# Strassen's block products for the gate projection too, in four of eleven groups of a ConvFFN, with the down projection in six parts instead of four

## The chip, the cores and the metric

One core of one Trainium2 chip runs the whole kernel. The metric is device microseconds of that core from the start to the end of one execution; lower is better. Times are medians of several runs, and each profile is of one execution.

## The reference, cut to what matters

A trunk of two layers, 512 tokens of width 1024 (D), float32. Each layer is a mixer and then a gated ConvFFN of width 2816:

```python
def gated_conv_ffn(x, w_gate, w_up, conv_w, conv_b, w_down):
    g = jnp.einsum('bsd,df->bsf', x, w_gate)
    g = causal_dwconv3(g, conv_w) + conv_b
    up = jnp.einsum('bsd,df->bsf', x, w_up)
    return jnp.einsum('bsf,fd->bsd', jax.nn.silu(g) * up, w_down)
...
        h = h + jnp.einsum('bse,ed->bsd', mix, w_out_even[i])
...
        hn = rms_norm(h, norm_ffn[layer])
        h = h + gated_conv_ffn(hn, w_ffn_gate[layer], w_ffn_up[layer], conv_ffn[layer],
                               b_conv_ffn[layer], w_ffn_down[layer])
    return rms_norm(h, final_norm)
```

The mixer of layer 0 joins a short gated convolution with causal pooling; that of layer 1 is a chunked spatial gate. Both begin with an RMS norm.

## The kernel before

**Arithmetic.** Each float32 operand is split into a high and a low part of a reduced-precision type (fp32r), and each product is three matmuls: high by high, high by low, low by high (`mm3`, L134). High parts are made by ScalarE (a copy), low parts by VectorE (a subtraction, `parts`, L127), or, in `summed` (L118), by ScalarE and an accumulating DMA that GpSimd issues. Weights come on SyncE's DMA queue into four raw buffers, and their halves take turns in five buffers of high and five of low parts.

**An FFN.** Its 2816 channels are 22 tiles of 128. The kernel goes through them in groups of two tiles, f and f + 1 (`hidden`, L711). A group makes the gate and the up projection of its tiles, and from them two activations: the gate gets a convolution over three tokens (`conv`, one ScalarE step L504 and two VectorE steps L506) and a silu (L512), and is multiplied by the up projection; `act` (L515) then splits it into a_hi (ScalarE, L261) and a_lo (VectorE, L263). Six pairs of such buffers take turns.

There are three forms of group:

- f = 0, `direct` (L532): gate and up of both tiles as 96 matmuls of 512 columns, on h not yet normalized, for the norm's factor r is not there when they begin. The factor is applied in `evacuate`: VectorE multiplies the gate by r (L555), GpSimd the silu (L558), VectorE puts in the up projection (L561). Ahead of that evacuation in the program stands `normalize` (L566) for four pairs of 128-row blocks. It makes the normalized halves hgh and hgl, and the sums of blocks (t23, t41) that Strassen's products need.
- f = 2, `direct` again, 96 matmuls of 512 columns, on the normalized halves (copies L553 on ScalarE instead of L555).
- all others, `seven` (L608): the up projection of two tiles by Strassen's seven block products, with 2 x 2 blocks of weights, rows and tokens. A product is 12 matmuls of 256 columns (L663), so 84 in all, where the direct form has 48 of 512 columns. The sums of weight blocks are made on VectorE (L631 to L639) and split (L619, L620). The gate of the same tiles is direct, 48 matmuls of 512 columns, between the first products. Results are gathered from PSUM by ScalarE copies (`keep`, L681) and VectorE additions (`add`, L684).

After each part of the tiles a down projection adds to the result, with all the part's activations as its inner dimension: `project` (L287) for layer 0, into h; a loop with `group8` (L948) for layer 1, into y. A part begins and ends eight PSUM banks, which VectorE adds into h or y (L306 and L923). The parts are

```python
    PARTS = ((0, 6), (6, 12), (12, 18), (18, 22))
```

so the order on TensorE is direct(0), direct(2), seven(4), down; seven(6), seven(8), seven(10), down; and so on.

**What sets the order.** The program is written in the order above, and a scheduler of the framework gives each engine its fixed list; an engine takes its list in order. PSUM has seven banks that matmuls take in turn and one more. The last inner steps of a group (`tail`) run bank by bank, the earlier ones inner step by inner step.

**Mixer 0's norm.** `Norm.rstd` (L194) sums squares over the 128 partitions by two matmuls of 512 columns with a matrix of ones (L200, L201), and takes the root and a reciprocal over 512 columns on VectorE. The FFN's norms use `rstd_tokens` (L206: eight one-column matmuls, then root and reciprocal of four columns) and `rstd_spread` (L215: four transposes that spread the columns over the partitions). `z_done` (L400) evacuates a group's projection and pools it.

Of the kernel before, what the change touches and what calls it, by code (L numbers as in the profile page):

```python
# [8 lines left out]
F32 = mybir.dt.float32  # L9
# [6 lines left out]
P = 128  # L16
# [14 lines left out]
def tile_trunk(ctx: ExitStack, tc: tile.TileContext, x, norm_mix, norm_ffn, final_norm,  # L31
# [16 lines left out]
    def aux_bank(name):  # L48
        return ps_aux.tile([P, 512], F32, tag="aux", name=name)
# [10 lines left out]
    small = cp.tile([P, LINE], F32, name="small")  # L60
    ones = small[:, :1]
    nc.gpsimd.memset(ones, 1.0)
    ones_r = cp.tile([P, P], F32R, name="ones_r")
    nc.gpsimd.tensor_copy(ones_r, ones.to_broadcast([P, P]))
# [20 lines left out]
    def params(layer, rows_, queue=nc.sync):  # L85
        rows = sum(n for _, _, n in rows_)
        pk = cp.tile([P, P], F32, tag="pk", bufs=1, name=f"pk{layer}")
        at, views = 0, {}
        for key, ap, n in rows_:
            queue.dma_start(pk[at : at + n, :], ap)  # L90
            views[key] = at
            at += n
        ps = aux_bank(f"prm_ps{layer}")
        nc.tensor.transpose(ps[:, :rows], pk[:rows, :], ident[:rows, :rows])
        sb = cp.tile([P, P], F32, tag=f"prm{layer}", name=f"prm{layer}")
# [21 lines left out]

    def summed(raw, a, b, name):  # L118

        hi = wp.tile([P, a, b], F32R, tag="whi", bufs=5, name=f"whi_{name}")  # L120
        lo = wp.tile([P, a, b], F32R, tag="wlo", bufs=5, name=f"wlo_{name}")
        nc.scalar.activation(lo, raw, AF.Copy, scale=-1.0)  # L122
        nc.gpsimd.dma_start(lo, raw, accum_op=ALU.add)  # L123
        nc.scalar.activation(hi, raw, AF.Copy)
        return hi, lo

    def parts(raw, a, b, name):  # L127
        hi = wp.tile([P, a, b], F32R, tag="whi", bufs=5, name=f"whi_{name}")
        lo = wp.tile([P, a, b], F32R, tag="wlo", bufs=5, name=f"wlo_{name}")
# [38 lines left out]
    class Norm:  # L168
# [13 lines left out]
        def square(self, k, order=lambda ins: ins):  # L182
            if self.n == 0:
                order(nc.scalar.activation(self.ssq, h[k], AF.Square))
            elif self.n == NK - 1 and self.apart:
                self.last = tp.tile([P, S], F32, tag="last", bufs=1, name=f"last_{self.name}")
                order(nc.scalar.activation(self.last, h[k], AF.Square))
            else:
                sq = tp.tile([P, S], F32, tag="sq", name=f"sq_{self.name}{k}")
                order(nc.scalar.activation(sq, h[k], AF.Square))  # L190
                nc.gpsimd.tensor_tensor(self.ssq, self.ssq, sq, ALU.add)
            self.n += 1

        def rstd(self):  # L194
            ps = aux_bank(f"ss_{self.name}")
            hi = tp.tile([P, S], F32R, tag="sq", name=f"ssh_{self.name}")
            lo = tp.tile([P, S], F32R, tag="sq", name=f"ssl_{self.name}")
            nc.scalar.activation(hi, self.ssq, AF.Copy)
            nc.vector.tensor_tensor(lo, self.ssq, hi.bitcast(F32), ALU.subtract)
            nc.tensor.matmul(ps, ones_r, hi, start=True, stop=False)  # L200
            nc.tensor.matmul(ps, ones_r, lo, start=False, stop=True)  # L201
            r = tp.tile([P, S], F32, tag="rstd", name=f"rstd_{self.name}")
            inv_sqrt(r, ps, S, self.name)
            return r

        def rstd_tokens(self):  # L206

# [139 lines left out]
    def mixer0():  # L347
        nonlocal prm0
        w = w_in_even[0]
        with tc.tile_pool(name="m0", bufs=1) as mp:  # L350
            prm_mix = params("mix", [("mix", rows_of(norm_mix[0]), NK)], nc.scalar)
            norm = Norm("m0", lambda k: prm_mix("mix", k))
            zchunks = {}
            xt = {}

# [12 lines left out]
            def turn(k):  # L368
# [2 lines left out]
                    nc.tensor.transpose(ps[:, t * P : (t + 1) * P], xt[k][:, t, :], ident)  # L371
                if k in raws:
                    raw, a, b, name = raws.pop(k)
                    hi = wp.tile([P, a, b], F32R, tag="whi", bufs=5, name=f"whi_{name}")
                    lo = wp.tile([P, a, b], F32R, tag="wlo", bufs=5, name=f"wlo_{name}")
# [21 lines left out]
            pooled = {}  # L397
            rstd = [None]

            def z_done(g, ps):  # L400
                if rstd[0] is None:
                    rstd[0] = norm.rstd()
                win = WINDOWS[g]
                z = mp.tile([P, S + LINE], F32, tag="z", bufs=2, name=f"z{g}")[:, :W]
                nc.gpsimd.memset(z[:, :PAD], 0.0)
                nc.scalar.copy(z[:, PAD:], ps)
# [80 lines left out]
    class Ffn:  # L487
# [110 lines left out]
        def moving(self, product, kp):  # L598
# [6 lines left out]
                return tuple(t[:, product - 6, :] for t in self.t23[kp])  # L605
            return tuple(t[:, {4: 0, 5: 1}[product], :] for t in self.t41[kp])

        def seven(self, f):  # L608
            layer, ap, n = self.layer, self.ap, f"{self.layer}_{f}"
            raws = ffn_weights(layer, f, [(key, half) for key in "ug" for half in range(2)])  # L610
# [1 line left out]
            stat = {}  # L612

            def pair(name):
                return [wp.tile([P, 2, 4, P], F32R, tag=f"w{x}", bufs=5, name=f"w{x}_{name}_{n}")
                        for x in ("hi", "lo")]

            def halves(hi, lo, src):
                nc.scalar.activation(hi, src, AF.Copy)  # L619
                nc.vector.tensor_tensor(lo, src, hi.bitcast(F32), ALU.subtract)  # L620

            def put(product, hi_lo, i):
                stat[product] = hi_lo[0][:, i], hi_lo[1][:, i]
# [22 lines left out]
                c = slice(i * P, (i + 1) * P)  # L646
                stat[product] = hi[:, :, c], lo[:, :, c]

            BANK = {1: "a", 6: "a", 7: "a", 4: "a", 5: "e", 3: "e", 2: "b"}
            banks, opened = {}, set()  # L650

            def multiply(product):
                at = BANK[product]
                if at not in banks:
                    banks[at] = mm_bank(f"u{at}{n}")
                ps = banks[at][:, :HALF]
                hi, lo = stat[product]
                for kp in range(NP):
                    b_hi, b_lo = self.moving(product, kp)
                    a_hi, a_lo = hi[:, kp, :], lo[:, kp, :]  # L660
                    for l, r, end in ((a_hi, b_hi, False), (a_hi, b_lo, False),
                                      (a_lo, b_hi, kp == NP - 1)):
                        nc.tensor.matmul(ps, l, r, start=at not in opened, stop=end,  # L663
                                         skip_group_check=True)
                        opened.add(at)
                return ps

            def gates(half):
                for k in PAIRS[half * 4 : half * 4 + 4]:
# [41 lines left out]
        def hidden(self, f, before=lambda i, j: None):  # L711
# [235 lines left out]

    def group8(name, ks, lhs, rhs, tail, on_done):  # L948
        banks = {}
        head = len(ks) - tail  # L950
# [43 lines left out]
```

## Time and profile before

| | |
| --- | --- |
| median of 3 runs | 1012.66 us (1012.38 to 1012.75) |
| the profiled execution's own time | 1013.46 us |
| its span between first and last instruction | 1011.5 us |
| mean granted TensorE clock | 0.997 |
| busy: TensorE, VectorE, ScalarE, GpSimd | 998.6, 612.6, 471.5, 90.0 us |
| direct(0) in layer 0 ends, direct(2) begins on TensorE | 171.21 us |
| direct(2) ends, seven(4) begins | 193.14 us |
| last matmul begins | 1003.57 us |

The profile gives the busy time of each engine as a share of the span; the chain of work that ended last, followed back from the end to what released each step; and groups of instructions by line, tile and shape. PE is TensorE, DVE VectorE, ACT ScalarE, POOL GpSimd and SP SyncE. In a timeline each row is the start, the length, the engine, the line, and what is written from what. Matmuls overlap, so the distance of their starts, not their length, is what one costs.

### The profile page before, as it was taken

Reading aid. Unit: us, or ns where it says so; the run is one execution under the profiler, and the core shown is the slowest. Engines: PE = TensorE matmul, PEld = TensorE weight load, DVE = VectorE, ACT = ScalarE, POOL = GpSimd, SP = SyncE. Lnnn points to the kernel's source line nnn. Section 1 sums busy time; section 2 is a strip of 40 time slices with the busy share of each in tenths; the row PEclk is TensorE's granted clock in tenths of the full one; section 3 lists DMA queues with packets and bytes.
Section 4 is the critical chain, followed back from the end, with each engine's and each line's share of the span. In section 5 each row is a group of like instructions: output and inputs, shape, how many; then the busy total and the mean of one; then the engine's idle time right before and its main releaser. Section 6 shows DMA issues by size and latency. Waiting matters only on the chain.

```text
span 1011.5 us, 13009 instructions
## 1 busy us (share of the span) xinstructions
PE 998.6 (99%) x5169; PEld 853.3 (84%) x5169; DVE 612.6 (61%) x882; ACT 471.5 (47%) x685; POOL 90.0 (9%) x101
## 2 busy tenths in 40 slices
PE   9999999999999999999999999999999999999997
PEld 6788888888998899889878888888888988998885
DVE  5997458864557366636833645396745654763667
ACT  6423446642454266236645444575425623650553
POOL 3141021200000000000300001111000000000000
PEclk9999999999999999999999999999999999999998
DMA  7432235442444344434333123354424433442432
GB/s 239 151 104 84 84 99 143 113 146 71 125 117 143 87 119 132 126 84 125 131 120 104 63 90 98 96 121 117 146 63 126 135 116 89 141 127 82 122 87 83
DMA packets 79303, 114.98 MB, mean 114 GB/s; under 512 B 4004, under 2 KB 53388, under 8 KB 79244
## 3 DMA queue, kind: packets, MB, share of 16 engines
q1 hardware_dynamic: 73580, 98.96, 30.7%
q0 software_dynamic: 4320, 13.63, 7.3%
q10 hardware_dynamic: 1344, 1.58, 0.5%
q8 instruction: 40, 0.66, 0.3%
q14 instruction: 19, 0.16, 0.1%
HBM read 98.42 MB, written 2.10 MB: 99 GB/s over the span
## 4 chain that ended last, share of the span: by engine, by line
PE 95%; DVE 3%; ACT 1%; issue 1%; DMA 1%; POOL 0%; DVEq 0%; ACTq 0%; POOLq 0%
PE ua L663 10%; PE g L135 7%; PE g L136 6%; PE g L137 6%; PE ue L663 5%; PE d L136 4%; PE dn L137 4%; PE dn L135 4%; PE d L137 4%; PE d L135 4%; PE dn L136 4%; PE gu L135 3%; PE gu L137 3%; PE gu L136 3%; PE ub L663 3%; PE u L135 1%
## 5 line engine op out<-in xcount | busy, mean ns | idle before, releaser
L135 PE MATMUL g<-hgh,whi_g 128*128 128x512 f32 x288 | 112.5, 391 | 0.0
L136 PE MATMUL g<-hgl,whi_g 128*128 128x512 f32 x288 | 112.5, 391 | 0.0
L137 PE MATMUL g<-hgh,wlo_g 128*128 128x512 f32 x288 | 112.1, 389 | 0.0
L130 ACT ACTIVATE whi_g<-raw_g 128x1024 fp32r<-128x1024 f32 x40 | 42.1, 1053 | 93.6 <-PE dn L137 57.3
L136 PE MATMUL d<-a_lo,whi_d 128*128 128x512 f32 x176 | 68.6, 390 | 0.0
L135 PE MATMUL dn<-whi_dn,a_hi 128*128 128x512 f32 x176 | 68.6, 390 | 0.0
L136 PE MATMUL dn<-wlo_dn,a_hi 128*128 128x512 f32 x176 | 68.5, 389 | 0.0
L506 DVE SCALAR_TENSOR_TENSOR c<-rows,prm,c 128x512 f32<-128x512 f32 x88 | 68.1, 793 | 0.6
L137 PE MATMUL d<-a_hi,wlo_d 128*128 128x512 f32 x176 | 68.5, 389 | 0.0
L137 PE MATMUL dn<-whi_dn,a_lo 128*128 128x512 f32 x176 | 68.3, 389 | 0.0
L135 PE MATMUL d<-a_hi,whi_d 128*128 128x512 f32 x176 | 68.3, 390 | 0.0
L131 DVE TENSOR_TENSOR wlo_g<-raw_g,whi_g 128x1024 fp32r<-128x1024 f32 x40 | 48.8, 1221 | 28.3 <-ACT whi_g L130 28.3
L137 PEld LDWEIGHTS g<-hgh,wlo_g 128*128 128x128 f32 x288 | 54.1, 188 | 11.9 <-DVE wlo_g L131 0.5
L123 POOL DMA_DIRECT2D wlo_u<-raw_u x18 | 15.4, 857 | 536.3 <-ACT wlo_u L122 200.1
L135 PEld LDWEIGHTS g<-hgh,whi_g 128*128 128x128 f32 x288 | 54.2, 188 | 10.3
L136 PEld LDWEIGHTS g<-hgl,whi_g 128*128 128x128 f32 x288 | 54.2, 188 | 9.8
L620 DVE TENSOR_TENSOR wlo_a<-raw_u,whi_a 128x512 fp32r<-128x512 f32 x18 | 12.5, 692 | 82.6 <-ACT whi_a L619 82.6
L681 ACT COPY kept<-ua 128x256 f32<-128x256 f32 x54 | 19.8, 367 | 74.3 <-PE ua L663 74.3
L131 DVE TENSOR_TENSOR wlo_d<-raw_d,whi_d 128x1024 fp32r<-128x1024 f32 x22 | 26.9, 1221 | 35.1 <-ACT whi_d L130 35.1
L131 DVE TENSOR_TENSOR wlo_dn<-raw_dn,whi_dn 128x1024 fp32r<-128x1024 f32 x22 | 26.8, 1220 | 35.1 <-ACT whi_dn L130 35.1
L923 DVE TENSOR_TENSOR y<-dn,y 128x512 f32<-128x512 f32 x32 | 22.1, 689 | 42.9 <-PE dn L137 42.9
L619 ACT ACTIVATE whi_s<-s 128x1024 fp32r<-128x1024 f32 x36 | 38.1, 1057 | 19.9 <-PE d L136 14.2
(326 smaller groups left out, 2756.7 us busy)
## 6 DMA issues: line engine op xcount, KB each, us to landing
raw_u<-in_w_ffn_up_dram SPq DMA_DIRECT2D x36, 512.0 KB
raw_g<-in_w_ffn_gate_dram SPq DMA_DIRECT2D x36, 512.0 KB
raw_d<-in_w_ffn_down_dram SPq DMA_DIRECT2D x22, 512.0 KB
raw_dn<-in_w_ffn_down_dram SPq DMA_DIRECT2D x22, 512.0 KB
wlo_u<-raw_u POOLq DMA_DIRECT2D x18, 512.0 KB, 4.6
raw_oe<-in_w_out_even_dram SPq DMA_DIRECT2D x8, 512.0 KB
raw_g<-in_w_ffn_gate_dram SPq DMA_DIRECT2D x16, 256.0 KB
raw_u<-in_w_ffn_up_dram SPq DMA_DIRECT2D x16, 256.0 KB
```

What stands on the lines that cost most here:

```text
L123: nc.gpsimd.dma_start(lo, raw, accum_op=ALU.add)
L130: nc.scalar.activation(hi, raw, AF.Copy)
L131: nc.vector.tensor_tensor(lo, raw, hi.bitcast(F32), ALU.subtract)
L135: nc.tensor.matmul(ps, lhs[0], rhs[0], start=start, stop=False)
L136: nc.tensor.matmul(ps, lhs[0], rhs[1], start=False, stop=False)
L137: nc.tensor.matmul(ps, lhs[1], rhs[0], start=False, stop=stop)
L506: nc.vector.scalar_tensor_tensor(c, t[:, i : S + i], prm("cf", i * NF + ft), c, op0=ALU.mult, op1=ALU.add)
L619: nc.scalar.activation(hi, src, AF.Copy)
L620: nc.vector.tensor_tensor(lo, src, hi.bitcast(F32), ALU.subtract)
L663: nc.tensor.matmul(ps, l, r, start=at not in opened, stop=end, skip_group_check=True)
L681: nc.scalar.copy(kept[:, i, :], ps)
L923: nc.vector.tensor_tensor(dst, ps, dst, ALU.add)
```

## The change

In groups 6, 10, 14 and 18 of each layer the gate is made by seven block products too (`both`): 168 matmuls of 256 columns in place of 84 of 256 and 48 of 512. Its block sums, their halves and its gathering from PSUM are like those of the up projection, and the products of gate and up alternate. `seven` remains for groups 4, 8, 12, 16 and 20, and shares its helpers with `both`. The parts become six, the first with tiles 0 and 1 alone; each of the others holds four tiles. The weight halves get six buffers instead of five, the activations four instead of six. In `group` and `group8` the part ahead of the tail may be empty. Mixer 0's norm takes the form with `rstd_tokens` and `rstd_spread`; the first two of its four groups are copied out of PSUM and pooled once the factor is there.

```diff
-        hi = wp.tile([P, a, b], F32R, tag="whi", bufs=5, name=f"whi_{name}")
-        lo = wp.tile([P, a, b], F32R, tag="wlo", bufs=5, name=f"wlo_{name}")
+        hi = wp.tile([P, a, b], F32R, tag="whi", bufs=6, name=f"whi_{name}")
+        lo = wp.tile([P, a, b], F32R, tag="wlo", bufs=6, name=f"wlo_{name}")
...
-        head = len(ks) - tail
+        head = max(0, len(ks) - tail)
...
-        def rstd(self):
...
-            norm = Norm("m0", lambda k: prm_mix("mix", k))
+            norm = Norm("m0", lambda k: prm_mix("mix", k), apart=True)
...
             def z_done(g, ps):
-                if rstd[0] is None:
-                    rstd[0] = norm.rstd()
...
+                if g == 0:
+                    norm.rstd_tokens()
+                elif g == 2:
+                    rstd[0] = norm.rstd_spread()
+                    z_pool(0)
+                    z_pool(1)
+                z_copy(g, ps)
+                if g > 1:
+                    z_pool(g)
...
-    PARTS = ((0, 6), (6, 12), (12, 18), (18, 22))
+    PARTS = ((0, 2), (2, 6), (6, 10), (10, 14), (14, 18), (18, 22))
+    BOTH = (6, 10, 14, 18)
...
-            self.acts[ft] = split(self.ap, s, f"a{self.layer}_{ft}", tag="a", bufs=6)
+            self.acts[ft] = split(self.ap, s, f"a{self.layer}_{ft}", tag="a", bufs=4)
...
+        def both(self, f):
...
+            w = self.unit(f"a11_{n}")
+            for i, key in enumerate("gu"):
+                self.halves(w[0][:, i], w[1][:, i], raws[key, 0][0][:, :, :P])
+                put(key, 1, w, i)
+            for key in "gu":
+                r0, r1 = raws[key, 0][0], raws[key, 1][0]
...
+                nc.vector.tensor_tensor(s12[:, 0], r0[:, :, P:], r1[:, :, P:], ALU.add)
+                nc.vector.tensor_tensor(s12[:, 1], s12[:, 0], r0[:, :, :P], ALU.subtract)
+                w = self.unit(f"s12{key}_{n}")
+                self.halves(*w, s12)
...
+                nc.vector.tensor_tensor(s34[:, 0], r0[:, :, :P], r0[:, :, P:], ALU.subtract)
+                nc.vector.tensor_tensor(s34[:, 1], r1[:, :, :P], s12[:, 1], ALU.subtract)
+                hi, lo = summed(*raws[key, 1])
...
+                w = self.unit(f"s34{key}_{n}")
+                self.halves(*w, s34)
...
+            for key, product in (("g", 1), ("u", 1), ("g", 5), ("g", 6), ("u", 5), ("u", 6),
+                                 ("g", 2), ("g", 7), ("u", 2), ("u", 7), ("g", 4), ("g", 3),
+                                 ("u", 4), ("u", 3)):
+                after(key, product, self.multiply(banks[key], f"{key}{n}", product,
+                                                  stat[key, product]))
+                if (key, product) == ("g", 4):
+                    s[1] = self.silu(self.conv(pads[1], f + 1), f + 1)
+                elif (key, product) == ("g", 3):
+                    s[0] = self.silu(self.conv(pads[0], f), f)
...
             elif f == 2:
                 self.direct(2, True, ((0, 1), (2, 3)), self.ch)()
+            elif f in BOTH:
+                self.both(f)
             else:
                 self.seven(f)
```

Here `after` copies a gate's or up's product out of PSUM into the padded rows or into `kept` (ScalarE), or adds it there (VectorE).

More of the change, by code (lines that the diff above doesn't have):

```diff
@@ L62, in tile_trunk @@
     nc.gpsimd.memset(ones, 1.0)
-    ones_r = cp.tile([P, P], F32R, name="ones_r")
-    nc.gpsimd.tensor_copy(ones_r, ones.to_broadcast([P, P]))
     def params0():
@@ L94, in params @@
         nc.tensor.transpose(ps[:, :rows], pk[:rows, :], ident[:rows, :rows])
-        sb = cp.tile([P, P], F32, tag=f"prm{layer}", name=f"prm{layer}")
+        sb = cp.tile([P, P], F32, tag="prm0" if layer == "0" else "prm1", name=f"prm{layer}")
         nc.vector.tensor_copy(sb[:, :rows], ps[:, :rows])
@@ L127, in parts @@
     def parts(raw, a, b, name):
-        hi = wp.tile([P, a, b], F32R, tag="whi", bufs=5, name=f"whi_{name}")
-        lo = wp.tile([P, a, b], F32R, tag="wlo", bufs=5, name=f"wlo_{name}")
+        hi = wp.tile([P, a, b], F32R, tag="whi", bufs=6, name=f"whi_{name}")
+        lo = wp.tile([P, a, b], F32R, tag="wlo", bufs=6, name=f"wlo_{name}")
         nc.scalar.activation(hi, raw, AF.Copy)
@@ L185, in square @@
             elif self.n == NK - 1 and self.apart:
-                self.last = tp.tile([P, S], F32, tag="last", bufs=1, name=f"last_{self.name}")
+                self.last = tp.tile([P, S], F32, tag="rstd", name=f"last_{self.name}")
                 order(nc.scalar.activation(self.last, h[k], AF.Square))
@@ L192, in square @@
             self.n += 1
-        def rstd(self):
[L195 to L204, printed above, removed]
         def rstd_tokens(self):
@@ L373, in turn @@
                     raw, a, b, name = raws.pop(k)
[L374 to L375 removed]
+                    hi = wp.tile([P, a, b], F32R, tag="whi", bufs=6, name=f"whi_{name}")
+                    lo = wp.tile([P, a, b], F32R, tag="wlo", bufs=6, name=f"wlo_{name}")
                     for i in range(a):
@@ L398, in mixer0, with z_copy, z_pool @@
             rstd = [None]
-            def z_done(g, ps):
-                if rstd[0] is None:
-                    rstd[0] = norm.rstd()
[L403 to L406, printed above, removed]
+            zs = {}
+            def z_copy(g, ps):
+                zs[g] = mp.tile([P, S + LINE], F32, tag="z", bufs=2, name=f"z{g}")[:, :W]
+                nc.gpsimd.memset(zs[g][:, :PAD], 0.0)
+                nc.scalar.copy(zs[g][:, PAD:], ps)
+            def z_done(g, ps):
+                if g == 0:
[7 more added lines that the diff above has]
+                    z_pool(g)
+            def z_pool(g):
+                win, z = WINDOWS[g], zs[g]
                 nc.vector.tensor_tensor(z[:, PAD:], z[:, PAD:], rstd[0], ALU.mult)
@@ L606, in moving, with multiply @@
             return tuple(t[:, {4: 0, 5: 1}[product], :] for t in self.t41[kp])
+        BANK = {1: "a", 6: "a", 7: "a", 4: "a", 5: "e", 3: "e", 2: "b"}
+        def multiply(self, banks, name, product, weights_):
+            at = self.BANK[product]
+            first = at not in banks
+            if first:
+                banks[at] = mm_bank(f"{name}{at}")
+            ps = banks[at][:, :HALF]
+            hi, lo = weights_
+            for kp in range(NP):
+                b_hi, b_lo = self.moving(product, kp)
+                a_hi, a_lo = hi[:, kp, :], lo[:, kp, :]
+                for l, r, end in ((a_hi, b_hi, False), (a_hi, b_lo, False),
+                                  (a_lo, b_hi, kp == NP - 1)):
+                    nc.tensor.matmul(ps, l, r, start=first, stop=end, skip_group_check=True)
+                    first = False
+            return ps
@@ L614, in pair @@
             def pair(name):
[L615 to L620, printed above, removed]
+                return self.unit(f"{name}_{n}")
+            halves = self.halves
             def put(product, hi_lo, i):
@@ L647, in seven @@
                 stat[product] = hi[:, :, c], lo[:, :, c]
-            BANK = {1: "a", 6: "a", 7: "a", 4: "a", 5: "e", 3: "e", 2: "b"}
-            banks, opened = {}, set()
+            banks = {}
             def multiply(product):
[L653 to L666, printed above, removed]
+                return self.multiply(banks, f"u{n}", product, stat[product])
             def gates(half):
@@ L949, in group8 @@
         banks = {}
-        head = len(ks) - tail
+        head = max(0, len(ks) - tail)
         order = [(i, j) for i in range(head) for j in range(8)]
```

48 lines of the change are left out of this document (added).

## The prediction

> **What bounds the kernel now.** I read the page's busy shares, then the chain of work that ended last, then the waits of the matrix engine, then the timelines around the end of the first FFN part.
>
> ```profile
> PE 998.6 (99%) x5169; PEld 853.3 (84%) x5169; DVE 612.6 (61%) x882; ACT 471.5 (47%) x685; POOL 90.0 (9%) x101
> ...
> PE 95%; DVE 3%; ACT 1%; issue 1%; DMA 1%; POOL 0%; DVEq 0%; ACTq 0%; POOLq 0%
> ```
>
> TensorE is busy 99% of the span and is 95% of the chain; VectorE has 39% to spare. The waits of TensorE, in full:
>
> ```profile
> PE wst L764 <- POOL ws L757: 1.5, 1, 1.5
> PE clock L56 <- DVE idle L53: 1.3, 1, 1.3
> PE z L135 <- ACT hgh L382: 1.0, 2, 0.8
> PE z L136 <- DVE hgl L384: 0.8, 1, 0.8
> PE xt_ps L371 <- DMA xt<-in_x_dram: 0.7, 1, 0.7
> ```
>
> None lies in an FFN. So fewer matmul microseconds pay in full, and a new wait costs in full. The last part and the way out (last matmul at 1003.57) keep their code.
>
> **Seven products for the gate.** Prices from the chain and the PE timeline:
>
> ```profile
> 206.94 1.43 PE ua L663 x12
> 208.37 1.44 PE ue L663 x12
> 209.81 1.44 PE ub L663 x12
> ...
> ```
>
> Products follow one another at 1.437 us for twelve 256-column matmuls, 0.1198 us each. 512-column ones start 0.2275 apart (171.21, 171.44, 171.67 below). A group's direct gate is 48 x 0.2275 = 10.91 us; its seven products are 84 x 0.1198 = 10.06. Saving 0.85 a group, with 4 groups in each of 2 layers **-6.8 us**. A row of the trace prices both forms, so the ends are narrow: -6.4 to -7.2 by reading the intervals a hundredth either way. The Trainium skill (TensorE: Matmul & The Clock Gate, Wait — 56ns, not 53.3ns?) counts a back-to-back matmul as its columns at 2.4 GHz plus 2.5 ns; by that estimate 48 x 0.2158 - 84 x 0.1092 is 1.19 a group and the sum would be 2.7 us lower. The trace has both forms longer, and decides.
>
> What this adds elsewhere must fit beside TensorE. From the DVE rows of such groups (128x1024 subtraction 1.22 us, 128x512 0.69, 256 columns 0.42, convolution step 0.79), a new group takes DVE 8 x 0.69 (sums) + 0.69 x 2 + 4 x 1.22 (low halves) + 4 x 0.79 + 6 x 0.42 (PSUM into rows) + 2 x 0.42 + 0.69 + 2 x 0.69 = 20.4 us, ACT some 16.4, against 168 x 0.1198 = 20.1 on PE. The group after it takes DVE 15.7 against PE 21.0, the down product of four tiles 10.4 against 21.9: 46.5 of 63 us. So DVE averages 74%, and I cost the steady state at 0. Its tight spot is the seven-product group behind a new one: ACT must copy the first product out 6.9 us after that group starts, behind about 26.9 us of queued work reckoned from the new group's start, where 27.0 are to be had. Ends: 0 to 1.5 us in each of eight places.
>
> **Six parts instead of four.** The number of down matmuls is the same. Two more parts in each layer add 16 PSUM evictions of 0.69 us on DVE a layer, beside other matmuls: 0. POOL's added accumulating copies (0.86 each, one for the gate's half per new group) and SP's reordered weight loads lie beside work too: DMA engines are about half busy. The short first part is another matter. Before, direct(2) stood behind direct(0):
>
> ```profile
> 170.99 0.39 PE L137 MATMUL gu<-hgh,wlo_u 128*128 128x512 f32 x1
> 171.21 0.39 PE L135 MATMUL gu<-hgh,whi_g 128*128 128x512 f32 x1
> 171.44 0.39 PE L136 MATMUL gu<-hgl,whi_g 128*128 128x512 f32 x1
> ```
>
> Those 96 matmuls (21.9 us, to 193.14) hid everything that VectorE, ScalarE and GpSimd then did: the rest of `normalize`, and direct(0)'s evacuation. The instruction order of the changed kernel has on PE direct(0), then the 48 matmuls of the down product of tiles 0 and 1, and only then direct(2). TensorE takes its queue in order, and direct(2)'s banks also come behind the down product's in the rotation of seven. So the down product asks for activation 0 at 171.2. When is it there? These rows of DVE, ACT and POOL give it:
>
> ```profile
> 157.04 1.41 DVE L571 SCALAR_TENSOR_TENSOR x<-h,prm,rstd_f 128x512 f32<-128x512 f32 x2 [4.10 <-ACT rstd_f L222]
> ...
> 175.34 0.69 DVE L555 TENSOR_TENSOR rows<-gu,rstd_f 128x512 f32<-128x512 f32 x1
> ...
> 184.39 0.68 DVE L561 TENSOR_TENSOR s<-gu,s 128x512 f32<-128x512 f32 x1
> ...
> 188.62 0.68 DVE L561 TENSOR_TENSOR s<-gu,s 128x512 f32<-128x512 f32 x1
> ```
>
> ```profile
> 179.84 1.28 ACT L512 ACT_TABLE_LOAD   x1
> 181.13 0.72 ACT L512 ACTIVATE s<-c,prm 128x512 f32<-128x512 f32 x1
> ...
> 185.10 0.63 ACT L261 ACTIVATE a_hi<-s 128x512 fp32r<-128x512 f32 x1 [1.05 <-DVE s L561]
> ```
>
> ```profile
> 181.94 1.98 POOL L558 TENSOR_TENSOR s<-s,rstd_f 128x512 f32<-128x512 f32 x1 [1.50 <-ACT s L512]
> ```
>
> From 157.04 DVE is full with `normalize` until the first evacuation at 175.34; then convolution, table load, silu, POOL's product, DVE's, and a_hi ends at 185.10 + 0.63 = 185.7. The changed order on DVE has the same `normalize` ahead of the same L555; down weights (two subtractions of 1.22) take the place of group 4's (0.69 + 1.22 + 2 x 0.69). So TensorE stands still from 171.2 to about 185.8, **14.6 us**. The low half comes at 187.0; activation 1 has silu at 185.75, POOL 1.58, DVE 0.68, ACT 0.62, low half at about 190.3, and 38 of the 48 matmuls remain then: 38 x 0.2275 = 8.65. direct(2) starts at about 199.0, instead of 171.2 + 10.9 with no wait. Loss 199.0 - 182.1 = **16.9 us**. Layer 1 has the same offsets (direct(2) from 673.02, its a_hi at 686.90: 13.9 behind, as in layer 0), so **+33.8** for both. Ends near it: direct(2)'s copies and convolution steps (1.05 on ACT, 1.40 and 1.78 on DVE) no longer stand between, which may give back 1.4 us a layer: +31; the two down weight copies now among `normalize`'s halves on ACT may cost 1.1 each layer: +36. Far end: the evacuation ahead of `normalize`, by its rows 0.69 + 0.72 + 2 x 0.79 + 1.28 + 0.72 + 1.98 + 0.68 + 0.63 = 8.3 us, or 7.0 with the table loaded earlier, and the same 2.3 behind it (16.9 - 14.6): +18.6 to +21.2.
>
> **The clock after the wait.** In the profile's windows, the stretch without matmuls at the end:
>
> ```profile
> 1005.00:1011.50 6.50, 0.00 (x0) 0.00 (x0) 2.40 (x8) 0.90 (x3) 0.00 (x0) 0.60 0.22 81
> 171.10:193.10 22.00, 22.00 (x100) 18.22 (x99) 22.00 (x34) 17.67 (x27) 6.98 (x6) 1.00 0.49 113
> ```
>
> ```profile
> 1.25 3.59 PE clock L56 x8
> ```
>
> The granted clock averages 0.60 there, against 1.00 in the full stretch, and in the opening eight 512-column matmuls (of bf16) take 3.59 us, 0.449 each, twice the 0.2275: idle TensorE loses its clock and starts at half rate. If the restart is at half rate for as long as that opening row, 3.6 us of unbroken matmuls, it loses about half of that, 1.65 us a layer: **+3.3** (ends 0 and +3.5). The Trainium skill speaks against the change in the same place (TensorE: Matmul & The Clock Gate, What's actually happening): some 3.4 us idle drop the clock to 1.2 GHz, and as long a sustained stretch restores it. By that estimate 1.7 us a layer, 3.4 in all; the opening row agrees, and no row before shows it after a mid-kernel wait.
>
> **Mixer 0's norm.** Eight one-column matmuls at about 0.22 apart (149.86 to 151.56 for the FFN's) and four transposes (0.35) replace two 512-column ones (0.46 together), +1.6 on PE if all is in the way; but the 0.79 and 0.80 waits at 31.0 and 33.67 lie there, and a DVE reciprocal over 512 columns (3.35 us) goes. I take **+0.5**, between 0 (filled waits) and +1.7, nearer the waits' rows.
>
> **Sum.** Own time of the profiled execution 1013.46 (span 1011.5) - 6.8 + 33.8 + 3.3 + 0.5 = 1044.3. That execution lies 0.8 above the median of 1012.66, so **1043.5 us** beside it.
>
> **Rivals.**
> 1. Clock kept: the wait costs its length only. For: the drop in the profile is after work has ended. Against: the opening row. 1043.5 - 3.3 = 1040.
> 2. Steady state late: the copy in the group behind a new one misses by 0.5 to 1.5 us eight times. For: 0.1 us of slack by my sum. Against: banks rotate over seven, and DVE averages 74%. 1047 to 1055.
> 3. Short wait: ScalarE and DVE are free enough that the evacuation comes first. 1012.7 - 6.8 + 18.6 to 21.2 + 0.5 = 1025 to 1028. Against: the order on DVE is fixed, with `normalize` ahead.
> 4. Faster, the other side: the down product of tiles 0 and 1 finds its activations ready, which takes 14.6 us of other matmuls ahead of it. It decides at a wait below (6.8 - 0.5) / 2 = 3.1 us a layer, less than silu, POOL's product and DVE's (0.72 + 1.98 + 0.68) alone; then about 1006. Against: the PE order has nothing between.
> 5. The change not doing what it says: if gates kept 512 columns in the four groups, the 6.8 would stay: 1050. The order shows 168 matmuls of 256 columns in each, so that goes with the range.
>
> **How the numbers follow.** Forecast 0.67, clock kept 0.12, late steady state 0.12, short wait 0.06, faster 0.03. 0.2%, 2 us, is about what a measurement of this kernel tells from no change. The range takes the unknown terms: -6.8 by 0.4, the wait 31 to 36, the clock 0 to 3.5, mixer 0 to 1.7: 1036 to 1051, which holds the forecast, the kept clock and half of the late case. Faster 0.03, same 0.01, slower 0.96.
>
> **What would show it.** TensorE's waits: two new ones, d0_00_0 on a_hi in layer 0, dn0_0 in layer 1, of 14 to 15 us each, with shorter ones behind; half clock in the matmuls after them; about 10.1 us for each gate's seven products; no waits over 0.5 us elsewhere in the FFN. I am wrong if TensorE does anything in that gap, if the evacuation comes well before 14 us, or if the products of the new groups wait.

## The result

The changed kernel takes **1042.45 us** (1041.18 to 1044.63, 4 runs) against 1012.7 (1012.38 to 1013.05, 4 runs): 1.0296 times the time before, 95% interval 1.0277 to 1.0315. The profiled execution took 1041.7 us, its span is 1040.0 and its mean granted clock 0.983.

The profile's busy shares and the chain by engine:

```profile
PE 999.5 (96%) x5475; PEld 865.6 (83%) x5475; DVE 660.4 (64%) x977; ACT 495.0 (48%) x725; POOL 91.9 (9%) x107
...
PE 91%; DVE 3%; issue 3%; DMA 2%; ACT 0%; SPq 0%; POOL 0%; DVEq 0%; POOLq 0%; ACTq 0%
```

TensorE is busy for 999.5 us, about as long as before, in a span that is 28.5 longer: what was added is idleness (the new groups shorten the busy time, and slow matmuls behind the waits lengthen it again). Where it idles, by its waits (us in total, times, longest):

```profile
PE dn L133 <- ACT a_hi L247: 14.9, 2, 14.3
PE d L133 <- ACT a_hi L247: 14.6, 2, 14.2
PE clock L56 <- DVE idle L53: 1.3, 1, 1.3
PE z L134 <- DVE hgl L370: 1.1, 2, 0.8
```

Two long waits, one in each layer's first down product, on a_hi, the high part of an activation. TensorE's timeline shows the one in layer 0; the bracket gives the idle time before the row and what ended it:

```profile
172.02 0.40 PE L135 MATMUL gu<-hgh,wlo_u 128*128 128x512 f32 x1
172.25 0.26 PE L92 MATMUL prm_ps<-ident,pk 112*128 112x112 f32 x1
186.71 1.22 PE L133 MATMUL d<-a_hi,whi_d 128*128 128x512 f32 x2 [14.20 <-ACT a_hi L247]
...
188.93 0.63 PE L134 MATMUL d<-a_lo,whi_d 128*128 128x512 f32 x1
189.36 0.63 PE L135 MATMUL d<-a_hi,wlo_d 128*128 128x512 f32 x1
...
190.85 1.22 PE L133 MATMUL d<-a_hi,whi_d 128*128 128x512 f32 x2 [0.44 <-ACT a_hi L247]
...
200.88 0.39 PE L135 MATMUL d<-a_hi,wlo_d 128*128 128x512 f32 x1
201.10 0.39 PE L133 MATMUL gu<-hgh,whi_g 128*128 128x512 f32 x1
```

direct(0) ends, 14.20 us pass, and the down matmuls then start 0.43 us apart instead of 0.2275; direct(2) begins at 201.10. The granted clock stands in the windows of the same stretch (window, its length, busy time of PE, PEld, DVE, ACT and POOL, clock, DMA share, GB/s):

```profile
175.00:176.00 1.00, 0.00 (x0) 0.00 (x0) 1.00 (x3) 1.00 (x3) 0.82 (x2) 0.80 0.00 0
176.00:177.00 1.00, 0.00 (x0) 0.00 (x0) 1.00 (x4) 1.00 (x3) 0.64 (x1) 0.50 0.93 162
...
192.00:193.00 1.00, 1.00 (x5) 0.79 (x4) 0.00 (x0) 0.00 (x0) 0.00 (x0) 0.67 0.00 0
193.00:194.00 1.00, 1.00 (x6) 0.83 (x5) 0.87 (x2) 0.00 (x0) 0.00 (x0) 1.00 0.00 0
```

The clock goes to half at 175.6, 3.1 us after TensorE went idle, and back to full at 192.7, 6.0 us after the first matmul behind the wait.

Both traces cut at the same places (starts of matmuls, and for mixer 1 the end of layer 0's last down matmul) give the whole account. "First part" is from direct(0)'s first matmul to direct(2)'s first; the 48 matmuls of the down product that now stand there (48 x 0.2275 = 10.9 us) are moved from the row below it, and the difference and the forecast allow for that.

| stretch | before | after | difference | forecast |
| --- | --- | --- | --- | --- |
| to direct(0) of layer 0 | 147.14 | 148.17 | +1.0 | +0.5 |
| first part, layer 0 | 24.07 | 52.93 | +17.9 | +18.55 |
| rest of the FFN, layer 0 | 330.91 | 316.68 | -3.3 | -3.4 |
| mixer 1 | 143.64 | 141.88 | -1.8 | 0 |
| first part, layer 1 | 27.26 | 55.57 | +17.4 | +18.55 |
| rest of the FFN, layer 1 | 330.55 | 317.00 | -2.6 | -3.4 |
| behind the last matmul, and outside the span | 9.89 | 9.47 | -0.4 | 0 |
| sum | 1013.46 | 1041.70 | +28.2 | +30.8 |

### The profile page after: what moved, and what is told of

It is laid out like the page before. It is cut to its first block, busy times and chain, and to the rows that moved or that the text cites. A ratio compares the mean times of both kernels' runs of the same rounds, so it can differ in the third digit from the quotient of the medians.

```text
span 1040.0 us, 13829 instructions
## 1 busy us (share of the span) xinstructions
PE 999.5 (96%) x5475; PEld 865.6 (83%) x5475; DVE 660.4 (64%) x977; ACT 495.0 (48%) x725; POOL 91.9 (9%) x107
## 4 chain that ended last, share of the span: by engine, by line
PE 91%; DVE 3%; issue 3%; DMA 2%; ACT 0%; SPq 0%; POOL 0%; DVEq 0%; POOLq 0%; ACTq 0%
PE d L133 4%; PE d L134 4%; PE dn L135 4%; PE dn L133 4%; PE dn L134 4%; PE d L135 4%; PE g L133 4%; PE g L134 4%; PE g L135 3%; PE gu L133 2%; PE gu L135 2%; PE gu L134 2%; PE v L133 1%; PE oo L135 1%; PE u L134 1%
## 5 line engine op out<-in xcount | busy, mean ns | idle before, releaser
L133 PE MATMUL d<-a_hi,whi_d 128*128 128x512 f32 x176 | 68.1, 398 | 14.6 <-ACT a_hi L247 14.6
L133 PE MATMUL g<-hgh,whi_g 128*128 128x512 f32 x160 | 62.5, 391 | 0.0
L134 PE MATMUL g<-hgl,whi_g 128*128 128x512 f32 x160 | 62.5, 391 | 0.0
L135 PE MATMUL g<-hgh,wlo_g 128*128 128x512 f32 x160 | 62.2, 389 | 0.0
L133 PEld LDWEIGHTS dn<-whi_dn,a_hi 128*128 128x128 f32 x176 | 33.4, 190 | 22.7 <-ACT a_hi L247 16.0
L133 PEld LDWEIGHTS d<-a_hi,whi_d 128*128 128x128 f32 x176 | 33.3, 191 | 22.6 <-ACT a_hi L247 15.9
L129 DVE TENSOR_TENSOR wlo_dn<-raw_dn,whi_dn 128x1024 fp32r<-128x1024 f32 x22 | 26.8, 1224 | 35.4 <-ACT whi_dn L128 35.4
L129 DVE TENSOR_TENSOR wlo_d<-raw_d,whi_d 128x1024 fp32r<-128x1024 f32 x22 | 26.8, 1224 | 35.4 <-ACT whi_d L128 35.4
L292 DVE TENSOR_TENSOR h<-d,h 128x512 f32<-128x512 f32 x48 | 32.7, 689 | 20.1 <-PE d L135 19.5
L247 ACT ACTIVATE a_hi<-s 128x512 fp32r<-128x512 f32 x44 | 27.4, 628 | 34.3 <-DVE s L792 13.3
L121 POOL DMA_DIRECT2D wlo_u<-raw_u x18 | 15.4, 858 | 306.6 <-ACT wlo_u L120 175.6
L129 DVE TENSOR_TENSOR wlo_u<-raw_u,whi_u 128x1024 fp32r<-128x1024 f32 x16 | 19.6, 1224 | 34.2 <-ACT whi_u L128 34.1
L135 PEld LDWEIGHTS dn<-whi_dn,a_lo 128*128 128x128 f32 x176 | 33.3, 189 | 8.5 <-DVE a_lo L249 1.3
L134 PEld LDWEIGHTS d<-a_lo,whi_d 128*128 128x128 f32 x176 | 33.6, 191 | 7.9 <-DVE a_lo L249 0.7
```

The source lines that it names most:

```text
L133: nc.tensor.matmul(ps, lhs[0], rhs[0], start=start, stop=False)
L134: nc.tensor.matmul(ps, lhs[0], rhs[1], start=False, stop=False)
L135: nc.tensor.matmul(ps, lhs[1], rhs[0], start=False, stop=stop)
L247: nc.scalar.activation(hi, src, AF.Copy, scale=scale)
L292: nc.vector.tensor_tensor(h[k], ps, h[k], ALU.add)
```

## The experiments

The theory: the loss is the uncovered wait, made by the place of the first down product, with VectorE's queue (`normalize`) setting its length and the clock adding to it; the new groups do save what their intervals say. The rivals: six parts cost by themselves; the new groups wait or cost; silu and GpSimd set the wait; the clock costs nothing. A third question came up on the way: whether the clock, or the order of the matmuls behind the wait, decides what follows it.

### The first down product one group later

```diff
+    HIDDEN = {0: (0, 2), 2: (4,)}
...
-                for f in range(a, b, 2):
+                for f in HIDDEN.get(a, range(a, b, 2)):
```

(in the loops of both layers, before `project` and before layer 1's down product).

> The changed kernel with one move: the down product of tiles 0 and 1 is issued behind direct(2) instead of ahead of it, so that the order is direct(0), direct(2), down(0,2), seven(4), down(2,6) and on. Six parts, the new groups and all buffers stay. Theory (the loss is the uncovered wait for the first activations, 17.95 us in layer 0 and 17.4 in layer 1 by the trace of the changed kernel): no wait over 1 us on a_hi is left and the time falls by about 35 to 1007 us (1005 to 1009), below the kernel before. Rival (six parts cost by themselves, through evictions, weight loads or less room for activations): at or above 1013.

Measured: 1006.95 us (1006.5 to 1008.5), 0.9951 of the kernel before (0.9937 to 0.9964). All waits of TensorE over the whole span:

```profile
PE xt_ps L357 <- DMA xt<-in_x_dram: 1.3, 1, 1.3
PE clock L56 <- DVE idle L53: 1.3, 1, 1.3
PE z L134 <- DVE hgl L370: 1.1, 2, 0.8
PE z L133 <- ACT hgh L368: 0.2, 1, 0.2
```

No wait is left in either FFN, and with nothing but the place of 48 matmuls in each layer moved, 35.5 us are gone. Six parts as such, their evictions and four activation buffers cost nothing that shows. That rival falls.

### The same parts without the new groups

```diff
-    BOTH = (6, 10, 14, 18)
+    BOTH = ()
```

> The changed kernel with no group of the new kind: groups 6, 10, 14 and 18 are seven-product groups with a direct gate again; six parts and the rest stay. Theory (the new groups save 0.85 us each by TensorE's intervals and wait for nothing): slower by 6 to 6.8 us, 1048.5 to 1049.3. Rival (part of the saving is lost to waits or reordering): slower by less than 4. Rival (the new groups cost more than they save): faster than the changed kernel.

Measured: 1048.42 us (1047.7 to 1050.04), 1.0358 of the kernel before (1.0344 to 1.0372): 6.0 us slower than the changed kernel by the medians, at the lower edge of the expected band. In the traces a pair of groups between two down products takes 41.99 us in both layers, against 41.15 in layer 0 and 41.31 in layer 1 of the changed kernel. So a new group saves 0.84 and 0.68 us, 6.1 for the eight. In layer 1 the scheduler's list breaks the product u5 off in the middle for g6, and 0.18 us of gaps stand at that place without a wait.

### Evacuation ahead of normalize

```diff
-                for kp in range(NP):
-                    self.normalize(kp)
-                rest()
+                rest()
+                for kp in range(NP):
+                    self.normalize(kp)
```

> The changed kernel with direct(0)'s evacuation issued ahead of normalize's program; the part borders stay. Theory (VectorE's queue, with normalize ahead, sets the wait): the wait on a_hi shrinks from 14.2 to about 9 us; as the low halves of the down weights now stand behind all of normalize on VectorE, at about 186, a wait on them follows, and direct(2) starts about 7 us earlier in each layer: 1026 to 1032 us. Rival (the chain of silu and GpSimd's product sets the wait, not the queue): within 3 us of 1042.

Measured: 1034.47 us (1034.33 to 1035.86), 1.0221 of the kernel before (1.0207 to 1.0235). It is 8.0 faster than the changed kernel, and 2.5 above the expected band. TensorE's waits:

```profile
PE dn L133 <- ACT a_hi L247: 8.1, 1, 8.1
PE d L133 <- ACT a_hi L247: 8.0, 1, 8.0
PE dn L134 <- DVE wlo_dn L129: 3.3, 1, 3.3
...
PE d L134 <- DVE a_lo L249: 0.9, 1, 0.9
```

The wait on a_hi falls from 14.2 and 14.3 to 8.0 and 8.1: VectorE's queue did set it, and about 8 us is what the bare chain of convolution, silu, GpSimd's product and split takes. What is late next is the low half of the down weights, behind all of `normalize` on VectorE: its first matmul starts at 187.2 in layer 0 and at 696.35 in layer 1, 15.4 us behind direct(0)'s end in both. In layer 0 14 matmuls stood ahead of it, most of them at half clock, and filled the time until then; direct(2) comes 5.6 us earlier behind direct(0) (23.2 instead of 28.85). In layer 1 only eight stood ahead, so that wlo_dn ended a second wait of 3.3 us, and the 40 matmuls behind it took 11.8 us instead of 9.1, for the granted clock stayed at 0.50 until 701.8; direct(2) comes only 1.1 us earlier (27.2 instead of 28.3). That is where the expectation, with 7 us in each layer, was too high, and here the half clock does lie on the path, with 2.7 us. (The scheduler's list has more of tile 0's matmuls ahead here too, so the waits tell more than the total.)

### Work in the wait

```diff
+                ps = aux_bank(f"fill{self.layer}")
+                still = ident.bitcast(BF16)
+                for i in range(112):
+                    nc.tensor.matmul(ps[:, :HALF], still[:, :P], still, start=i == 0,
+                                     stop=i == 111)
```

(behind direct(0)'s matmuls).

> The changed kernel with 112 matmuls of 256 columns added on TensorE (bf16, on the identity matrix, into a spare bank that nobody reads) between direct(0) and the down product of tiles 0 and 1: some 12 to 13 us of work that fills the wait and computes nothing that is used. Theory (after the idle 14 us TensorE runs at half rate for about 6 us, of which 1.0 to 1.4 us a layer is on the path): the matmuls behind the wait start at 0.23 us intervals and the time falls by 2 to 3, to 1039.5 to 1040.5. Rival (the clock costs nothing, the slow matmuls wait for operands anyway): within 0.7 of 1042.5.

Measured: 1038.97 us (1038.9 to 1039.24), 1.0263 of the kernel before (1.0249 to 1.0277), 3.5 faster than the changed kernel with 224 matmuls more, and half a microsecond below the expected band. The first a_hi comes no earlier (14.5 us behind direct(0)'s end, as in the changed kernel), but direct(2) does: 27.1 us behind it instead of 28.85 in layer 0, 26.5 instead of 28.3 in layer 1. That looks like a half clock of 1.75 us a layer. But TensorE's timeline in layer 0 doesn't fit:

```profile
182.84 2.35 PE L809 MATMUL fill<-ident 128*128 128x256 bf16 x20
187.25 1.75 PE L133 MATMUL d<-a_hi,whi_d 128*128 128x512 f32 x5 [2.06 <-ACT a_hi L247]
188.79 0.63 PE L134 MATMUL d<-a_lo,whi_d 128*128 128x512 f32 x1
189.22 0.63 PE L135 MATMUL d<-a_hi,wlo_d 128*128 128x512 f32 x1
...
191.93 0.40 PE L134 MATMUL d<-a_lo,whi_d 128*128 128x512 f32 x1
192.16 0.85 PE L133 MATMUL d<-a_hi,whi_d 128*128 128x512 f32 x3
```

After 2.06 us of idleness the rate still fell to half, some 1 us into the down product, and came back 3.4 us later; layer 1, with an idle time as long, stayed at 1.00 in every window. And the order of the matmuls (the scheduler's list) differs: with the filling in front, the scheduler put 14 matmuls of tile 0 ahead of the first of tile 1, against 7 in the changed kernel. So this run changed two things, and the next two take them apart.

### The same filling with the old list, the new list without filling

The order of the first down product's 48 matmuls is written out, for the first kernel as the changed kernel has it (with 128 matmuls in the wait), for the second as the filled kernel had it (and no filling):

```diff
+            inorder(nc.tensor.matmul(banks[j], l[term == 2], r[term == 1],
+                                     start=left[j] == 5, stop=left[j] == 0))
```

(one matmul for each entry of the list).

> The changed kernel with 128 matmuls of 256 columns in the wait, as in e4_fill but some 1.8 us longer, and with the order of the first down product's 48 matmuls written out in each layer as the changed kernel has it (7 of tile 0's, then the first of tile 1's). In e4_fill the scheduler had put 12 to 14 of tile 0's ahead, so its 3.5 us mix two causes. New theory (with 7 matmuls ahead, the second a_hi, 4.15 us behind the first, ends the next wait at either clock, so that the half clock costs only what it slows behind that: 0.9 us in layer 0, 0.4 or less in layer 1): 1041.1 to 1041.9 us. Rival (the half clock costs 1.75 us in each layer, as e4_fill was first read): 1038.5 to 1039.3.

> The changed kernel without any filling, with the order of the first down product's matmuls written out as e4_fill had it (12 of tile 0's ahead in layer 0, 14 in layer 1); the half clock stays. New theory (the order, not the clock, made most of e4_fill's gain): direct(2) some 1.8 us earlier in layer 0 and 1.3 in layer 1, 1038.7 to 1040 us. Rival (the clock made it): within 0.7 of 1042.45.

Measured: with filling and the old list 1043.3 us (1041.76 to 1043.43), 1.03 of the kernel before (1.0285 to 1.0314), no faster than the changed kernel and above both expected bands; with the new list and no filling 1039.68 us (1039.44 to 1040.24), 1.0269 (1.0255 to 1.0283), inside the new theory's band. **So the order made most of the gain, and the first reading of the filled kernel falls.** The run with the trace is the fastest of the first kernel's four, 1041.76 us at a clock of 0.998, inside the new theory's band; the other three took 1043.3 to 1043.43 at 0.996, and no trace shows where their clock was lower. That trace shows why the order counts, in TensorE's timeline of layer 0:

```profile
186.67 0.73 PE L152 MATMUL d<-a_hi,whi_d 128*128 128x512 f32 x2 [0.32 <-ACT a_hi L272]
187.87 0.50 PE L152 MATMUL d<-a_lo,whi_d 128*128 128x512 f32 x1 [0.47 <-DVE a_lo L274]
...
190.83 0.73 PE L152 MATMUL d<-a_hi,whi_d 128*128 128x512 f32 x2 [1.53 <-ACT a_hi L272]
```

At the full clock (0.998 over the run) TensorE is done sooner with the seven matmuls that it may do, and then waits 1.53 us for tile 1, at 190.83; at half clock it waited 0.44, until 190.85. The half clock was hidden by the second wait, except behind it: direct(2) comes 28.1 us behind direct(0) instead of 28.85 in layer 0, and 28.3 in both kernels in layer 1. In the second kernel, seven more matmuls (7 x 0.2275 = 1.6 us) fit into the wait for tile 1: 27.4 and 26.8 us.

The cost of the half clock is not the same in each trace. The kernel without the new groups has the old list and no filling either, but there the clock was back 3.9 us after the first down matmul of layer 0 instead of 6.0, and direct(2) comes 28.1 and 28.6 us behind direct(0). Against the 28.1 and 28.3 at the full clock that is 0 and 0.3 us lost, where the changed kernel lost 0.75 and 0. With the new list the filling takes off another 0.7 us by the medians (1038.97 against 1039.68), 0.3 in each layer of the traces.

### The old norm of mixer 0

The edit puts `rstd`, `ones_r` (in the mixer's pool) and the old `z_done` back into the kernel of the first experiment.

```diff
-            norm = Norm("m0", lambda k: prm_mix("mix", k), apart=True)
+            norm = Norm("m0", lambda k: prm_mix("mix", k))
+            norm.ones_r = mp.tile([P, P], F32R, name="ones_r")
...
             def z_done(g, ps):
-                if g == 0:
-                    norm.rstd_tokens()
...
+                if rstd[0] is None:
+                    rstd[0] = norm.rstd()
```

> The kernel of e1_defer with mixer 0's norm and pooling as before the change (two 512-column matmuls with ones, reciprocal over 512 columns, each projection pooled as it is evacuated). Theory (the new norm costs about 1 us: the FFN of layer 0 starts at 148.2 to 148.7 us instead of 147.1): 1005.5 to 1006.3, about 1 below e1_defer's 1006.95, and the FFN starts at about 147.2. Rival (the start's scatter, not the norm): 1006.5 to 1007.5, FFN start as in e1_defer.

Measured: 1006.39 us (1005.89 to 1006.82), 0.9939 of the kernel before (0.9927 to 0.9952). The FFN of layer 0 starts at 147.35 instead of 148.43, so the new norm costs 1.1 us in this pair of traces. The medians differ by 0.56, between the two expectations, and the two intervals overlap: the times alone don't show it. The traces together do: the FFN of layer 0 starts at 147.1 to 147.4 in the three kernels with the old norm (before, this one and the last below), and at 147.7 to 148.7 in the ten with the new one.

### A fifth new group, and all nine

```diff
-    BOTH = (6, 10, 14, 18)
+    BOTH = (4, 6, 10, 14, 18)
```

> The kernel of e1_defer with a fifth group of the new kind in each layer, group 4, which now stands behind the down product of tiles 0 and 1. Theory (each such group saves 0.85 and its load fits beside the matmuls): 1.7 us below e1_defer, 1005.2. Rival (the down product of 48 matmuls ahead of it is too short a cover for its sums and halves): a wait in group 4 and no gain, 1007 to 1010.

Measured: 1005.12 us (1004.31 to 1005.32), 0.9925 of the kernel before (0.9912 to 0.9937), with no wait in an FFN. Group 4 takes 20.15 us in both layers instead of 20.99. 48 down matmuls are cover enough.

```diff
+    BOTH = tuple(range(4, 22, 2))
```

> The kernel of e1_defer with all nine groups from 4 to 20 of the new kind in each layer, so that in four places one of them follows another. Theory by TensorE's intervals alone: 10 more groups by 0.85, 998.4. VectorE's load would be 20.4 + 20.4 + 10.4 of 62 us a period, which still fits on average. Rival (a new group behind a new one waits, as VectorE needs 20.4 us for 20.1 of matmuls and the seven pairs of halves go through six buffers): waits in groups 8, 12, 16 and 20, 1000 to 1015.

Measured: 1006.76 us (1004.83 to 1007.45), 0.9939 of the kernel before (0.9926 to 0.9951): nothing gained over five groups. TensorE's waits:

```profile
PE g_18e L624 <- DVE rows L692: 3.1, 2, 2.5
...
PE u_10a L624 <- ACT kept L682: 1.0, 1, 1.0
PE g_6e L624 <- DVE rows L692: 0.7, 1, 0.7
...
PE g_10e L624 <- DVE rows L692: 0.2, 1, 0.2
```

Here the rival holds, though the waits stand in groups 6, 10 and 18 and not in 8, 12, 16 and 20, where it had them: products of later new groups wait for banks that VectorE or ScalarE hasn't emptied. VectorE's work still fits on average, 46.3 of 62.3 us in the window of two new groups and a down product in layer 0, but not at each moment. All but 0.5 us of these waits are in layer 1; a pair of new groups takes 40.4 us in layer 0 (41.1 the last), and 40.6 to 43.3 in layer 1.

### The old first part

```diff
-    PARTS = ((0, 2), (2, 6), (6, 10), (10, 14), (14, 18), (18, 22))
+    PARTS = ((0, 6), (6, 10), (10, 14), (14, 18), (18, 22))
...
-            self.acts[ft] = split(self.ap, s, f"a{self.layer}_{ft}", tag="a", bufs=4)
+            self.acts[ft] = split(self.ap, s, f"a{self.layer}_{ft}", tag="a", bufs=6)
```

(and `bufs=5` for the halves of weights).

> The changed kernel with the old first part: parts (0,6), (6,10), (10,14), (14,18), (18,22), groups 6 to 18 by fours of the new kind, six activation buffers, and five buffers of weight halves to make room. Theory (only the first border matters, and direct(2) and seven(4) cover direct(0)'s evacuation): within 1.5 us of e1_defer, 1005.5 to 1008.5. Rival (five weight buffers starve the new groups): new waits in groups 6 to 18 and over 1009.

Measured: 1009.39 us (1008.47 to 1009.94), 0.9968 of the kernel before (0.9956 to 0.998). The long waits are gone here too, a second way to the same end. It is 2.4 above the first experiment, outside the theory's band, but the rival's waits aren't there either: the longest in the FFN is 0.3 us. A pair of groups takes 41.47 us instead of 41.15 in layer 0, and 41.45 to 42.01 instead of 41.31 in layer 1, 2.7 us over the eight, with 0.29 of gaps in most pairs where the list breaks a half of the gate off for matmuls of u5 and u2 and then resumes. With five buffers the scheduler orders the matmuls otherwise; why such a break costs 0.1 to 0.2 us isn't settled.

### Together

Old norm, the first down product behind direct(2), new groups 4 to 18 in layer 0 and 4, 6, 10, 14, 18 in layer 1:

```diff
+    BOTH = ((4, 6, 8, 10, 12, 14, 16, 18), (4, 6, 10, 14, 18))
...
-            elif f in BOTH:
+            elif f in BOTH[self.layer]:
```

> The down product of tiles 0 and 1 behind direct(2), the old norm of mixer 0, and groups of the new kind where e6_defer_five and e7_defer_all showed no wait: 4, 6, 8, 10, 12, 14, 16 and 18 in layer 0; 4, 6, 10, 14 and 18 in layer 1. Theory (0.77 us for each of three more groups than e6_defer_five, and 0.6 to 1 for the norm): 1002.1 us (1001.5 to 1003). Rival (the gains are not additive, for VectorE is late somewhere else): 1003.5 or more.

Measured: 1003.72 us (1002.4 to 1004.8), 0.9916 of the kernel before (0.9903 to 0.993): faster than both kernels. The profiled execution took 1002.4 us, within the band, with no wait in an FFN; the median lies 0.7 above the band and 0.2 above the rival's limit. So by the times the gains may not quite add up, as the rival has it, while the trace shows no place where VectorE is late. The five runs scatter by 2.4 us at clocks of 0.998 and 0.999; why isn't settled.

## Why the prediction was right, step by step

- **The order and the wait.** The decisive step, that the down product of tiles 0 and 1 stands uncovered ahead of direct(2), held: 14.20 and 14.30 us were measured for 14.6. First evacuation at 176.36 for 175.34 and a_hi's split at 186.03 for 185.10 are the forecast rows moved by the 1.0 us of mixer 0. VectorE's rows in the changed kernel:

```profile
176.36 0.69 DVE L555 TENSOR_TENSOR rows<-gu,rstd_f 128x512 f32<-128x512 f32 x1
...
180.76 2.36 DVE L129 TENSOR_TENSOR wlo_d<-raw_d,whi_d 128x1024 fp32r<-128x1024 f32 x2
...
185.32 0.68 DVE L561 TENSOR_TENSOR s<-gu,s 128x512 f32<-128x512 f32 x1
```

  The two down weight halves do stand in the place of group 4's.
- **What follows the wait.** At the full clock and with the same list direct(2) came 28.1 and 28.3 us behind direct(0); less 10.9, wait and rest lose 17.2 and 17.4 us, where 16.9 was forecast. Seven matmuls stood ahead of tile 1, not the ten that the forecast allowed, so 41 x 0.2275 = 9.3 us remained behind the second wait. Both layers together: 0.8 us too little.
- **The clock: the step that was mis-sized.** TensorE did fall to half rate, as forecast from the window at the end and the opening row. But of the 3.3 us that this was to cost, 0.75 showed, all in layer 0 (0.3, all in layer 1, in the trace without the new groups). The step added the lost half of 3.6 us to the path as if TensorE had work throughout; for the first 4.15 us, up to the second a_hi, it had seven matmuls (1.6 us at the full clock), and the slower rate used up waiting time. Where 40 matmuls had all their operands, in layer 1 with the evacuation first, 2.7 us did show. (The sum has a slip besides: half of the opening row's 3.6 us is 1.8 a layer, not 1.65.) The Trainium skill (TensorE: Matmul & The Clock Gate, What's actually happening) gives some 3.4 us for the drop and as much for the return. The drop took 3.1 and 3.9 us in the changed kernel, the return behind unbroken matmuls 2.9 to 4.2 over the traces, so they agree in size; what the sentence can't tell is whether the slow time lies on the path.
- **The new groups.** Forecast 6.8, measured 5.9 in the two rest stretches and 6.0 by undoing them. Layer 0 is as forecast; in layer 1 the broken product takes back 0.16 of each 0.84.
- **Six parts, the steady state.** Costed at 0, and 0 in the first experiment. The rival of a late steady state did not come: ScalarE's copy ended 6.5 us after the start of the group behind a new one in all eight places, where 6.9 were to be had, so the slack was 0.4 us for the 0.1 reckoned, and no such wait is in the trace. Only with all nine groups new does it begin.
- **Mixer 0** cost 1.0 for 0.5: of the 1.6 us that the one-column matmuls and transposes could add, little went into waits. Those of z fell only from 1.8 us to 1.3.
- **Mixer 1**, costed at 0, became 1.8 us shorter, and this is the one thing that no step of the prediction names. Before, its transposes of the spatial weights waited 1.5 us for GpSimd, which waited for their DMA; that wait isn't in the trace after. The eleven kernels of the experiments spend 141.9 to 142.6 us there, those without the new groups, with the old norm or with the old numbers of buffers (the old first part, 142.4) too, so no one of these is what made it. In the trace before, GpSimd began on the weights 5.6 us after their load was issued and took 1.99 us for them, in all others 4.2 to 5.3 and 1.1 to 1.2. That is the only trace of the kernel before, and the cause stays open.

The errors nearly cancel, and that much of the closeness is luck: by the profiled executions the clock term was 2.55 too high and mixer 1 and the end 2.2, the rest of the first parts was 0.8 and mixer 0 0.5 too low, and the new groups saved 0.9 less than forecast. Together 2.5 us, 30.8 forecast and 28.2 measured; the medians, 1043.5 and 1042.45, are 1.05 apart.

## What to carry to other kernels

A part's border is a join: the product behind it needs what the group just ahead has to finish, so ask of each border which matmuls stand between the two; here 48 matmuls a layer, one group too early, cost nearly six times what the better arithmetic of eight groups saved. Read the length of such a wait from the whole queue of the engine that makes the operand (14.2 us), not from the bare chain (8.0), and ask what is late next before a slower clock or a faster engine is added to the path. A filling or an edit can change the scheduler's list elsewhere: compare the order before a gain is put down to what was meant.

## What the runs showed of the hardware

The granted clock takes two values in these traces, 1.00 and 0.50; at 0.50 matmuls of 512 columns start 0.43 us apart instead of 0.2275. It changes on a grid of its own: in the clock records of all the traces every stretch between two changes is a whole multiple of 3.413 us (17.07 and 13.65 us at half clock in the changed kernel, five and four times; 3.41 in the filled one). So the delays differ from trace to trace. In the four kernels with an unfilled wait it fell 2.6 to 4.7 us after the last matmul. It returned 2.9 to 4.2 us after the first one behind the wait where these were unbroken (layer 1 of the changed kernel 3.3, the kernel with the new list 4.2 and 2.9). Where a second wait of some 0.45 broke them, it returned after 6.0 (layer 0 of the changed kernel), 3.9 and 5.4 us (the kernel without the new groups). In the first and the last of these three the whole break lies in the last step of the grid before the return, so such a break did not hold the return up there. An idle time of 2.06 us went with a drop in layer 0 of the filled kernel, about 1 us after work had resumed, and with none in layer 1; on that grid all of it fell into one step in layer 0, and 1.9 us of it in layer 1.

Breaking a product off in the middle for another cost 0.1 to 0.2 us at a break, without a wait that the profile names.
